# Selection columns inside another constant, and a 32-byte gap behind each page of on-chip memory

## The chip, the cores and the metric

The kernel runs on one core of a Trainium2 chip. It is one program for the core's five engines: TensorE (PE for its matmuls, PEld for its weight loads), VectorE (DVE), ScalarE (ACT), GpSimd (POOL) and SyncE (SP), which here only issues DMAs. The metric is device time in microseconds (us) of one execution, given as the median of several runs. A profile is one execution taken by the hardware profiler.

## The reference

A two-layer backbone over 1,024 latent tokens of width 1,024, with 256 context tokens ahead of them. All arrays are float32.

```python
for i in range(2):
    shift, scale, gate = split(silu(c) @ ada_w[i] + ada_b[i], 3)
    h = rmsnorm(x, norm_g[i]) * (1 + scale) + shift
    if i == 0:   # windowed grouped-query attention, 16 query heads, 4 key heads of 128
        q, k, v, z = split(h @ w_in)            # 1024 -> 2048 + 512 + 512 + 2048
        q, k = rope(q), rope(k)
        o = softmax([sink, q @ k_ctx, q @ k_window]) @ [v_ctx, v_window]   # |i - j| <= 128
        y = (o * silu(z)) @ w_out               # 2048 -> 1024
    else:        # convolution module
        a, gl, z = split(h @ w_in + b_in, 3)    # 1024 -> 3 * 2048
        u = depthwise_conv31(a * sigmoid(gl)) + dw_b
        y = (silu(layernorm(u) * g + b) * silu(z)) @ w_out
    x = x + gate * y
return rmsnorm(x) * final_g
```

## The kernel before, in words

Every large matrix product is done in the `float32r` type of TensorE with the operands split into a high and a low part: `hi = round(full)`, `lo = full - hi`. One product is then three matmuls into the same accumulator: high with high, high with low, low with high (`mm3`). In each of them one operand is stationary (128 by 128, loaded ahead of the matmul) and the other streams through (mostly 128 partitions by 512 columns, 2,048 bytes in each partition).

Nearly all of these operands live in 45 **pages**: buffers of 1,024 float32 values (4,096 bytes) in each of the 128 partitions, handed out by `pg = Pages(pgpool, 45, "page", 1024)`. Six smaller buffers of 528 values (2,112 bytes), `hp = Pages(pgpool, 6, "half", 528)`, hold intermediate rows. A freed page goes to the end of the line of free ones, so that the same page holds one after another a raw weight block (`wraw`), its high or low part (`whi`, `wlo`), a part of the normalised input (`hh`, `hl` in the first layer, `h2h`, `h2l` in the second), queries, keys, values, probabilities (`p`), or a part of the gated branch output (`ozh`, `ozl`, `gs`) or of an output weight block (`woh`, `wol`).

```python
def alloc(self, dt, shape=None, name="pg"):
    i = self.free_.popleft()
    t = self.pool.tile([P] + list(shape or [self.words]), dt, tag=f"{self.tag}{i}",
                       name=f"{name}_{self.tag}_{self.count}", bufs=1)
```

A page gets its place in a partition when its tag is used for the first time, behind what was placed before it; each buffer takes a multiple of 32 bytes. Constants come first (`ctile`): the identity `ident`, `vt` (128 by 128, a table of per-channel vectors, of which columns 0 to 111 are used), `sel` (128 by 2: two columns of zeros and ones), `sink`, `nsink`, `ones`, `dww`, then `pthi` and `ptlo` (the transposed probabilities), small vectors, and then halves and pages.

`sel` is read by TensorE alone. In `ada_cols(pr)`, which runs four times within the first 60 us, four small matmuls add the four rows of a modulation product and turn them into columns: `PE.matmul(cps[:, 2 * i:2 * i + 2], rw[0:5, i * P:(i + 1) * P], sel[0:5], ...)`.

The stages in order: modulation products (`ada_mm`, with weights `araw`) and the first projections, bound by loads; the attention heads, each with its projections in the gaps (`gemm_half`: stationary `whi` or `wlo`, streaming `hh` or `hl`); the output projection of the first layer (`proj_attn`: stationary `ozh` or `ozl`, streaming `woh` or `wol`); the second layer's input projection (`b_mm`: stationary `whi` or `wlo`, streaming `h2h` or `h2l`) with the convolution on VectorE, GpSimd and ScalarE beside it; its output projection (`proj_out`: stationary `gs`, streaming `woh` or `wol`). The order of instructions on each engine comes from the tile framework's scheduler; TensorE's is the program's own.

Of the kernel before, what the change touches and what calls it, by code (L numbers as in the profile page):

```python
# [9 lines left out]
F32 = mybir.dt.float32  # L10
# [4 lines left out]
P = 128  # L15
# [38 lines left out]
class Pages:  # L54


    def __init__(self, pool, n, tag, words):
        self.pool, self.tag, self.words = pool, tag, words
        self.free_ = deque(range(n))
        self.at = {}  # L60
        self.count = 0

    def alloc(self, dt, shape=None, name="pg"):
        if not self.free_:
            raise RuntimeError(str([t[1].name for t in self.at.values()]))
        i = self.free_.popleft()
        self.count += 1
        t = self.pool.tile([P] + list(shape or [self.words]), dt, tag=f"{self.tag}{i}",
                           name=f"{name}_{self.tag}_{self.count}", bufs=1)
        self.at[id(t)] = (i, t)  # L70
        return t

# [22 lines left out]
def backbone_kernel(  # L95
# [23 lines left out]
    def nm(s):  # L119
        uid[0] += 1  # L120
        return f"{s}_{uid[0]}"
# [21 lines left out]
    def ctile(shape, dt, name):  # L143
        return cpool.tile(shape, dt, tag=name, name=name, bufs=1)
# [15 lines left out]

    ident = ctile([P, P], F32, "ident")
    vt = ctile([P, P], F32, "vt")
    sel = ctile([P, 2], F32, "sel")
    sink = ctile([P, NH], F32, "sink")
    nsink = ctile([P, NH], F32, "nsink")
    ones = ctile([P, P], F32, "ones")
# [1038 lines left out]
    for t in ("pthi", "ptlo"):  # L1205
        f = cpool.tile([P, 5, 528], F32, tag=t, name=nm("ubuf"), bufs=1)
# [520 lines left out]
```

## Time and profile before

| | us |
|---|---|
| median of 3 runs | 1757.55 |
| lowest and highest of them | 1756.67, 1760.27 |
| span of the profiled execution, first to last instruction | 1752.9 |
| PE busy in that span (8,420 matmul records) | 1720.7 |
| PEld, DVE, ACT, POOL busy | 1424.8, 1148.3, 889.4, 895.4 |

The page of the profile gives no time for the profiled execution but its span; the median lies 4.65 us above it, and that is taken as what lies around a span. "Idle before" in a row is idle time of the engine just before the instructions of that row, with what ended it. A matmul's record lasts longer than the time from its start to the next one's, since matmuls follow each other in a pipeline; so rates are read from the starts. In the chain of work that ended last, a row gives the start, the length and after "x" the number of instructions, so that length over number is the time for one.

### The profile page before, as it was taken

Reading aid. Unit: us, or ns where it says so; the run is one execution under the profiler, and the core shown is the slowest. Engines: PE = TensorE matmul, PEld = TensorE weight load, DVE = VectorE, ACT = ScalarE, POOL = GpSimd, SP = SyncE. Lnnn points to the kernel's source line nnn. Section 1 sums busy time; section 2 is a strip of 40 time slices with the busy share of each in tenths; the row PEclk is TensorE's granted clock in tenths of the full one; section 3 lists DMA queues with packets and bytes.
Section 4 is the critical chain, followed back from the end, with each engine's and each line's share of the span. In section 5 each row is a group of like instructions: output and inputs, shape, how many; then the busy total and the mean of one; then the engine's idle time right before and its main releaser. Section 6 shows DMA issues by size and latency. Waiting matters only on the chain.

```text
span 1752.9 us, 23877 instructions
## 1 busy us (share of the span) xinstructions
PE 1720.7 (98%) x8420; PEld 1424.8 (81%) x8420; DVE 1148.3 (66%) x2079; ACT 889.4 (51%) x1548; POOL 895.4 (51%) x705
## 2 busy tenths in 40 slices
PE   7999999999999999999999999999999999999997
PEld 4788888888888888888888888888888888788886
DVE  6755564556546563656315189999999999867823
ACT  7555553445345444545334355554665564466731
POOL 0245654566636565653101267998898888130300
PEclk9999999999999999999999999999999999999999
DMA  9334443444334542436777733011121202377971
GB/s 313 107 82 139 136 133 85 145 147 145 100 105 143 152 142 87 136 119 203 279 250 239 241 90 105 13 54 31 43 79 36 91 30 79 120 254 243 325 264 48
DMA packets 195324, 242.45 MB, mean 138 GB/s; under 512 B 11798, under 2 KB 126790, under 8 KB 195204
## 3 DMA queue, kind: packets, MB, share of 16 engines
q1 hardware_dynamic: 188516, 230.10, 40.3%
q10 hardware_dynamic: 6688, 10.83, 2.6%
q8 instruction: 66, 1.08, 0.3%
q14 instruction: 54, 0.44, 0.1%
HBM read 188.70 MB, written 41.69 MB: 131 GB/s over the span
## 4 chain that ended last, share of the span: by engine, by line
PE 86%; DMA 5%; DVE 3%; POOL 2%; ACT 2%; issue 2%; SPq 1%; ACTq 0%; POOLq 0%; DVEq 0%
PE psg L89 44%; PE pss L89 22%; PE pso L89 19%; DMA araw_page<-in_ada_w_dram 1%; POOL rope_half L89 1%; DMA low_page<-in_conv_w_out_dram 1%; DMA rope_half<-rope_half 1%; SPq L89 1%; DMA low_page<-in_attn_w_out_dram 1%; DMA wolC<-low_page 1%; DVE mask_page L89 1%; ACT p_page L89 0%; POOL wlo_page L89 0%; POOL low_page L89 0%; DMA wraw_page<-in_attn_w_in_dram 0%
## 5 line engine op out<-in xcount | busy, mean ns | idle before, releaser
L89 POOL TENSOR_TENSOR odd_half<-odd_half,prod_half 128x513 f32<-128x513 f32 (+2 forms) x252 | 312.8, 1250 | 24.2 <-ACT prod_half L89 11.0
L89 PE MATMUL psg<-hh_page,whi_page 128*128 128x512 f32 x600 | 237.6, 396 | 0.0
L89 PE MATMUL psg<-hh_page,wlo_page 128*128 128x512 f32 x600 | 236.9, 395 | 0.0
L89 PE MATMUL psg<-hl_page,whi_page 128*128 128x512 f32 x600 | 236.8, 395 | 0.0
L89 POOL TENSOR_TENSOR wlo_page<-wraw_page,whi_page 128x1024 fp32r<-128x1024 f32 x70 | 173.1, 2475 | 104.1 <-ACT whi_page L89 83.2
L89 ACT ACTIVATE prod_half<-ubuf,dww 128x513 f32<-128x513 f32 (+2 forms) x252 | 165.1, 674 | 107.3 <-POOL odd_half L89 105.1
L89 POOL TENSOR_SCALAR p_page<-p_page,sc 128x640 f32<-128x640 f32 (+1 forms) x128 | 100.8, 787 | 224.4 <-DVE sc L89 208.7
L89 PE MATMUL psg<-h2h_page,whi_page 128*128 128x512 f32 x464 | 183.9, 396 | 0.0
L89 PE MATMUL psg<-h2h_page,wlo_page 128*128 128x512 f32 x464 | 183.0, 394 | 0.0
L89 PE MATMUL psg<-h2l_page,whi_page 128*128 128x512 f32 x464 | 182.4, 393 | 0.0
L89 DVE SCALAR_TENSOR_TENSOR pss<-ubuf,dww,pss 128x512 f32<-128x512 f32 (+3 forms) x270 | 172.3, 670 | 0.1
L89 DVE SCALAR_TENSOR_TENSOR pss<-ubuf,wsum,pss 128x512 f32<-128x512 f32 (+3 forms) x270 | 171.7, 670 | 0.2
L89 DVE TENSOR_TENSOR ptlo<-pss,pthi 128x640 fp32r<-128x640 f32 (+1 forms) x144 | 103.3, 717 | 64.0 <-ACT pthi L89 62.8
L89 ACT ACTIVATE p_page<-p_page,sc 128x641 f32<-128x641 f32 (+1 forms) x128 | 102.7, 802 | 74.1 <-DVE sc L89 69.7
L89 ACT ACTIVATE pthi<-pss 128x640 fp32r<-128x640 f32 (+1 forms) x144 | 88.6, 615 | 91.7 <-PE pss L89 86.3
L89 PEld LDWEIGHTS psg<-hh_page,wlo_page 128*128 128x128 f32 x600 | 112.9, 188 | 26.3
L89 PEld LDWEIGHTS psg<-hh_page,whi_page 128*128 128x128 f32 x600 | 113.0, 188 | 20.8 <-DVE kvc_page L89 0.2
L89 PEld LDWEIGHTS psg<-hl_page,whi_page 128*128 128x128 f32 x600 | 112.9, 188 | 20.7
L89 ACT ACTIVATE whi_page<-wraw_page 128x1024 fp32r<-128x1024 f32 x88 | 92.6, 1053 | 69.0 <-PE psg L89 25.5
L89 PE MATMUL pso<-h2l_page,whi_page 128*128 128x512 f32 x304 | 119.9, 394 | 0.0
L89 PE MATMUL pso<-h2h_page,whi_page 128*128 128x512 f32 x304 | 119.8, 394 | 0.0
L89 PE MATMUL pso<-h2h_page,wlo_page 128*128 128x512 f32 x304 | 119.6, 394 | 0.0
(244 smaller groups left out, 4105.2 us busy)
## 6 DMA issues: line engine op xcount, KB each, us to landing
wraw_page<-in_conv_w_in_dram SPq DMA_DIRECT2D x48, 512.0 KB
wraw_page<-in_attn_w_in_dram SPq DMA_DIRECT2D x40, 512.0 KB
wol_page<-wolA SPq DMA_DIRECT2D x32, 512.0 KB
wo_page<-in_attn_w_out_dram SPq DMA_DIRECT2D x32, 512.0 KB
wo_page<-in_conv_w_out_dram SPq DMA_DIRECT2D x32, 512.0 KB
wol_page<-wolC SPq DMA_DIRECT2D x32, 512.0 KB
rope_half<-rope_half ACTq DMA_DIRECT2D x80, 128.0 KB
araw_page<-in_ada_w_dram SPq DMA_DIRECT2D x32, 256.0 KB
```

What stands on the lines that cost most here:

```text
L89: r = f(*a, **k)
```

## The change

The two columns of `sel` become columns 112 and 113 of the constant `vt`, which were unused. The DMA that fills them and the sixteen small matmuls that read them name `vt` instead of `sel`. And when a page's tag is used for the first time, a buffer of 8 float32 values (32 bytes), which nothing reads or writes, is placed behind the page.

```diff
@@ class Pages, __init__
         self.count = 0
+        self.shifted = set()
@@ class Pages, alloc
                            name=f"{name}_{self.tag}_{self.count}", bufs=1)
+        if self.tag == "page" and i not in self.shifted:
+            self.shifted.add(i)
+            self.pool.tile([P, 8], F32, tag=f"gap{i}", name=f"gap_{i}", bufs=1)
         self.at[id(t)] = (i, t)
@@ backbone_kernel
-    sel = ctile([P, 2], F32, "sel")
+    sel = vt[:, 112:114]
```

No instruction is added, removed or moved on any engine, and each waits for the same semaphores as before. What differs in the instructions is the one name. On SyncE's queue, at the program's start, before (`sel` is the selection constant, `crow` the condition vectors, `araw` the modulation weights):

```order
3 L89 DMA ident<-in_k_ident_dram 128x128
4 L89 DMA crow_half_75<-in_norm_g_dram 16x128
5 L89 DMA sel<-in_k_sel_dram 128x2
6 L89 DMA araw_page_92<-in_ada_w_dram 128x2x256 x2
7 L89 DMA araw_page_93<-in_ada_w_dram 128x2x256 x2
```

and now (the line number of the recording helper is 93 instead of 89, and buffer numbers are shifted by the gap buffers):

```order
3 L93 DMA ident<-in_k_ident_dram 128x128
4 L93 DMA crow_half_74<-in_norm_g_dram 16x128
5 L93 DMA vt<-in_k_sel_dram 128x2
6 L93 DMA araw_page_92<-in_ada_w_dram 128x2x256 x2
7 L93 DMA araw_page_94<-in_ada_w_dram 128x2x256 x2
```

The DMA stands in the same place with another destination. What the change does move is addresses. The built programs place the buffers so (bytes within a partition):

| | before | after |
|---|---|---|
| `pthi`, `ptlo` | 4832, 16096 | 4800, 16064 |
| first page, second, third, fourth | 34848, 41056, 45152, 49248 | 34816, 41056, 45184, 49312 |
| pages at a multiple of 64 | 0 of 45 | 23 of 45 |
| pages 32 behind a multiple of 64 | 45 of 45 | 22 of 45 |
| halves at a multiple of 64 | 0 of 6 | 5 of 6 |
| pages by address modulo 256, with 0, 32, 64, 96, 128, 160, 192, 224 | 0, 26, 0, 9, 0, 6, 0, 4 | 7, 6, 5, 6, 5, 4, 6, 6 |
| end of the last page | 227616 | 228992 |

Of the program's 8,362 matmuls 6,055 stream 512 columns. Over these, the addresses of the streaming operand and of its own stationary operand compare as follows:

| of 6,055 matmuls with 512 columns | before | after |
|---|---|---|
| streaming operand starts at a multiple of 64 | 0% | 50.5% |
| the two operands' addresses are equal modulo 256 | 30.6% | 11.2% |
| the two operands' addresses differ modulo 64 | 0.8% | 51.0% |

## The prediction, made before the changed kernel was run

> **What bounds the kernel now.** The head of the profile's page and its line of shares in the chain of work that ended last come first.
>
> ```profile
> span 1752.9 us, 23877 instructions
> PE 1720.7 (98%) x8420; PEld 1424.8 (81%) x8420; DVE 1148.3 (66%) x2079; ACT 889.4 (51%) x1548; POOL 895.4 (51%) x705
> PE   7999999999999999999999999999999999999997
> PEclk9999999999999999999999999999999999999999
> PE 86%; DMA 5%; DVE 3%; POOL 2%; ACT 2%; issue 2%; SPq 1%; ACTq 0%; POOLq 0%; DVEq 0%
> ```
>
> TensorE's matmuls are busy for 1720.7 of 1752.9 us, at the full clock, in every slice but the first and the last, and 86% of the chain is theirs. No other engine is above 66%, and the weight loads fill 81%. So the time is set by how soon one matmul can follow another. That is read next from the chain, whose long pieces are unbroken runs of matmuls with 512 columns: start, length, engine, output, line and count.
>
> ```profile
> 977.41 44.47 PE pss L89 x192
> 1047.61 33.33 PE psg L89 x144
> 1500.09 27.78 PE psg L89 x120
> ```
>
> Length over count is 231.6, 231.5 and 231.5 ns. The clock cannot explain any difference from run to run here, since it is granted in full throughout. But single stretches differ. The timeline of TensorE around 984 us (part of the first piece above) and around 831 us gives starts and lengths:
>
> ```profile
> 984.00 0.39 PE L89 MATMUL pss<-woh_page,ozl_page 128*128 128x512 f32 x1
> ...
> 986.94 0.39 PE L89 MATMUL pss<-woh_page,ozh_page 128*128 128x512 f32 x1
> 831.02 0.40 PE L89 MATMUL psg<-wol_page,ozh_page 128*128 128x512 f32 x1
> ...
> 833.35 0.40 PE L89 MATMUL psg<-woh_page,ozl_page 128*128 128x512 f32 x1
> ```
>
> In the first stretch 13 starts take 2.94 us, 226.2 ns each; in the second 10 take 2.33 us, 233.0 ns each. The operation is the same, and so are shape, operand kinds and neighbours. What differs is where the operands lie. In the first stretch all four pages (two of streaming weights, two stationary) start 32 bytes behind a multiple of 256. In the second the streaming pages do so too, but both stationary ones start 96 behind one. So 6.8 ns, 3%, hangs on the lowest bits of addresses when they stay the same for several matmuls. That is the only thing this change touches.
>
> The slowest regular spacing is in the input projection of the second layer:
>
> ```profile
> 1379.49 0.40 PE L89 MATMUL psg<-h2l_page,whi_page 128*128 128x512 f32 x1
> 1379.72 0.40 PE L89 MATMUL psg<-h2h_page,wlo_page 128*128 128x512 f32 x1
> 1379.96 0.39 PE L89 MATMUL psg<-h2h_page,whi_page 128*128 128x512 f32 x1
> ```
>
> The second start to the third is 0.24 us, against 0.23 from the first to the second.
>
> **The change part by part.** No instruction is added, removed or moved, so every term is a change in duration.
>
> *VectorE, ScalarE, GpSimd.* The convolution reads one buffer at many offsets, tap by tap, and the tile view shows what an offset does to a duration (minimum, median, maximum in ns):
>
> ```profile
> L89 ACT ACTIVATE prod_half<-ubuf,dww x49: 707/727/732, 1170.0 to 1259.7; 128x513 f32<-128x513 f32 x49
> L89 DVE SCALAR_TENSOR_TENSOR pss<-ubuf,dww,pss x27: 734/740/750, 1169.5 to 1218.1; 128x512 f32<-128x512 f32 x27
> L89 PE MATMUL pso<-sel,arow_half x32: 245/247/268, 16.4 to 59.6; 5*128 5x2 f32 x32
> ```
>
> The taps start at offsets that differ by 4 or 8 bytes, so that starts on, 32 behind and anywhere between multiples of 64 are among them; the medians lie within 2% of both ends on VectorE and 3% on ScalarE. GpSimd has no such row; it takes the same 0. What hides an error of 2% is that these engines are not the bound. In the convolution's stages it can be seen by the windows view (length, then busy time and count of PE, PEld, DVE, ACT and POOL, clock, DMA share, GB/s):
>
> ```profile
> 0.00:40.00 40.00, 31.85 (x126) 18.31 (x127) 23.91 (x42) 28.83 (x35) 0.92 (x7) 0.96 0.98 308
> 990.00:1480.00 490.00, 490.00 (x2136) 398.47 (x2135) 447.33 (x722) 278.21 (x401) 407.11 (x299) 1.00 0.20 61
> ```
>
> TensorE is busy for all of 490.00 us; VectorE has 42.67 us to spare, 9.5% of its work. Term: 0. Without this cover 2% of 447.33 would be 8.9 us.
>
> *The selection columns.* Thirty-two of the recorded small matmuls, at 245 to 268 ns in the row above, all within the first 60 us. If the operand's new place changed each by as much as they differ among themselves (23 ns), it would be 0.7 us either way; taken 0.
>
> *Loads.* In the second window above the transfer engines are busy for 0.20, and a load there has slack. In the first 40 us they are busy for 0.98 and the loads lead. The chain's share for the window from 0 to 45 us, and the pieces of three such loads:
>
> ```profile
> by line: DMA araw_page<-in_ada_w_dram 53.9%; SPq L89 27.8%; issue 5.9%; PE pso L89 4.8%; DVE alo_page L89 2.7%; DVE hf_page L89 1.8%; ACT hh_page L89 1.7%; ACTq L89 0.1%; ACT ahi_page L89 0.1%; DVE hl_page L89 0.1%; DVEq L89 0.0%
> 15.91 7.07 DMA araw_page<-in_ada_w_dram
> 27.19 6.19 DMA araw_page<-in_ada_w_dram
> 33.40 5.10 DMA araw_page<-in_ada_w_dram
> ```
>
> 53.9% of 45 us is 24.3 us of transfers into pages. Their pieces spread by 7.07 − 5.10 = 2 us though every destination is 32 behind a multiple of 64. I take 0 for the new destinations and ±2 us as bounds.
>
> *TensorE, the one term with a size.* Of the 6,055 matmuls with 512 columns, the streaming and the stationary operand now start equal modulo 256 in 30.6%, and afterwards in 11.2%: 19.4 points, 1,176 matmuls. If each of them loses what the steady stretches show, 1,176 × 6.8 ns = 8.0 us are added. That is the upper bound. The lower one comes from the chain's own pieces: by the addresses, the piece at 977.41 has 42% of its matmuls with equal operands and the piece at 1047.61 has 18%, and they run at 231.6 and 231.5 ns. Where the classes alternate from matmul to matmul, as they mostly do, the share does nothing. So 0 to 8 us; I take 2, because the long mixed pieces are the nearer rows, and the changed kernel's sequences are mixed still more. Only a steady run, like the one at 984 us, can lose the full 6.8 ns.
>
> The bounds do not cover what is new: half of the streams (50.5%) start at a multiple of 64, and half of the pairs (51.0%) differ by an odd multiple of 32. In the trace of before nearly all 512-column streams start 32 behind one, and only 0.8% of the pairs differ modulo 64. Those are the modulation products, whose stationary condition columns lie 0, 16 or 48 behind a multiple of 64:
>
> ```profile
> 30.27 0.40 PE L89 MATMUL pso<-alo_page,c 128*4 128x512 f32 x1
> ...
> 33.05 0.40 PE L89 MATMUL pso<-alo_page,c 128*4 128x512 f32 x1
> ```
>
> Twelve starts in 2.78 us are 231.7 ns each, just the common rate. That speaks for no new price, though with a stationary operand of only 4 columns. The weight loads, mean 188 ns in the row below (instructions, busy us, mean ns), fit under 231 with 43 ns to spare, so a load that is slower by a fifth still stays hidden.
>
> ```profile
> L89 PEld LDWEIGHTS psg<-hh_page,whi_page 128*128 128x128 f32 x600 | 113.0, 188 | 20.8 <-DVE kvc_page L89 0.2
> ```
>
> The Trainium skill, in "SBUF — State Buffer", section "Specifications (TRN2)", gives 16-byte lines in that memory, with a penalty for crossing into a new one; both the old and the new starts lie on such a line, so by it alone nothing would change. The two rates at 984 and 831 us, whose starts are all on such lines, show that this is not the whole of it.
>
> Sum: 0 + 0 + 0 + 2 us on a span of 1752.9 us. The median of the runs lies 4.65 us above that span, at 1757.55, and I carry these over unchanged: 1757.55 + 2 = 1759.6 us.
>
> **The rivals.** A difference of 0.2%, 3.5 us, is about what a measurement of this kernel can tell from none; the three runs of before span 3.6 us.
>
> *Half of the streams run at the better rate (faster).* If the common loss comes from starting 32 behind a multiple of 64 (nearly every 512-column stream did), those that now start at one run at 226.2 instead of 231.5 ns: 5.3 ns × 3,058 = 16 us, 1741.5. If the alternation frees both halves, it is twice that, 32 us, 1725.5. For it: 226.2 occurs, so the engine can do it, and no other work stands in the way. Against it: in the stretch at 984 us the streams start 32 behind and yet run at the best rate.
>
> The Trainium skill, in "TensorE: Matmul & The Clock Gate", section "Back-to-back issue gap", gives N/2.4 + 2.5 ns for isolated warm matmuls, which is 215.8 ns for 512 columns; no stretch here reaches it. Half of the streams at that rate would make this rival's gain an estimated 48 us.
>
> *Pairs that differ by 32 collide (slower).* Two operands that lie 64 apart modulo 256 cost 6.8 ns more than equal ones; a half step could cost more again. Priced at the slowest regular spacing, 0.24 us to the two digits shown and 241 by the trace's nanoseconds, 9.5 ns × 3,088 (51.0% of 6,055) is 29 us: 1786.9. It decides from 1.1 ns for each such pair, where it passes 3.5 us. For it: closeness in the low bits is what helps, and the change takes it away. Against it: the modulation products, at 231.7 ns.
>
> *The addresses even out (no change).* Successive matmuls already mix four classes modulo 256, and mixing eight gives the same mean: 1757.6 us.
>
> **How the numbers follow.** The forecast, with its own range from 1757.5 to 1765.6, has 0.40: between a loss of 0 and of 8 us, about half of it on each side of 3.5 us (0.22 slower, 0.18 same). The even mixture has 0.05, all same. The better rate has 0.33, since a new class of streams is half of the work and nothing but its untested rate speaks on it. The collision has 0.22, less because one row of pairs that differ shows no price. Faster 0.33; same 0.18 + 0.05 = 0.23; slower 0.22 + 0.22 = 0.44. The likeliest single figure is 1759.6. The range must take in most of both outer cases: down to 1728, just short of both halves gaining, and up to 1786, just short of the full collision. What lies outside is the last of either, about 0.1 at each end.
>
> **What would show it.** Right: the same counts of instructions, VectorE, ScalarE and GpSimd busy within 1% of before, PE at full clock, and long pieces of the chain between 231.5 and 233 ns per matmul, with steady stretches of 226 become rare. The better rate would show in those pieces as 226 to 229 ns, above all where streams start at multiples of 64; the collision as 234 ns and more where the operands differ by an odd multiple of 32. Idle time on TensorE of more than now, or a first 45 us that ends over 2 us earlier or later, would say that the loads or the other engines do feel the addresses, and my zeros were wrong.

## The result, and the profile after

The changed kernel takes 1756.3 us (median of 12 runs, 1753.8 to 1759.96), the kernel before 1757.31 us beside it (12 runs, 1754.05 to 1760.51). The ratio is 1.0001, with a 95% interval from 0.9994 to 1.0009; it is not simply the quotient of these two medians, which is 0.9994, the lower end of that interval. Either way no change can be told. The forecast was 1759.6 us, 2 us more than before. "Same", the outcome that came, had the smallest of its three chances, 0.23.

The head of the page of the changed kernel, to be held against the lines of before:

```profile
span 1753.1 us, 23877 instructions
PE 1722.7 (98%) x8420; PEld 1423.6 (81%) x8420; DVE 1144.2 (65%) x2079; ACT 889.6 (51%) x1548; POOL 895.1 (51%) x705
PEclk9999999999999999999999999999999999999999
```

The counts are the same. VectorE, ScalarE and GpSimd are busy for the same time within 0.4%, as the zeros for them had it. TensorE has 2 us more. The long pieces of its chain (start, length, engine, output, line, count), in the changed kernel:

```profile
975.77 44.42 PE pss L93 x192
1045.92 33.35 PE psg L93 x144
1499.17 27.83 PE psg L93 x120
1579.81 27.88 PE pss L93 x120
```

Before they were 44.47, 33.33, 27.78 and, below, 27.78 us. So the first is 0.1% shorter, the others are 0.1 to 0.4% longer; for one matmul that is 231.4, 231.6, 231.9 and 232.3 ns. Two more pieces of before say where it stood in time:

```profile
457.02 14.00 PE psg L89 x72
...
1580.50 27.78 PE pss L89 x120
```

and the piece in the changed kernel that answers to the first of them:

```profile
455.48 14.00 PE psg L93 x72
```

The changed kernel is 1.54 us ahead at 457 us, 0.69 us ahead at 1580, and 0.2 us behind at the end. From 457 us to the end it lost 1.7 us, and a quicker start covered it. Whether that start belongs to the change is asked below.

In each profile some 5,950 matmuls with 512 columns have a start that follows at once on another's. Their mean spacing, worked out from all these starts, is 231.73 ns before and 231.98 ns after. 0.25 ns × 5,950 is 1.5 us, where the prediction put 2.

### The profile page after: what moved, and what is told of

Read it like the earlier page. It is cut to its first block, busy times and chain, and to the rows that moved or that the text cites. A ratio compares the mean times of both kernels' runs of the same rounds, so it can differ in the third digit from the quotient of the medians.

```text
span 1753.1 us, 23877 instructions
## 1 busy us (share of the span) xinstructions
PE 1722.7 (98%) x8420; PEld 1423.6 (81%) x8420; DVE 1144.2 (65%) x2079; ACT 889.6 (51%) x1548; POOL 895.1 (51%) x705
## 4 chain that ended last, share of the span: by engine, by line
PE 86%; DMA 6%; DVE 2%; POOL 2%; ACT 2%; issue 1%; SPq 1%; ACTq 0%; POOLq 0%; DVEq 0%
PE psg L93 45%; PE pss L93 22%; PE pso L93 19%; DMA araw_page<-in_ada_w_dram 1%; POOL rope_half L93 1%; DMA low_page<-in_conv_w_out_dram 1%; DMA wraw_page<-in_attn_w_in_dram 1%; DMA rope_half<-rope_half 1%; SPq L93 1%; DMA low_page<-in_attn_w_out_dram 1%; DMA x_page<-in_x_dram 0%; ACT p_page L93 0%; POOL wlo_page L93 0%; DMA wo_page<-in_conv_w_out_dram 0%; DMA wolC<-low_page 0%
## 5 line engine op out<-in xcount | busy, mean ns | idle before, releaser
L93 PE MATMUL psg<-hh_page,wlo_page 128*128 128x512 f32 x600 | 236.4, 394 | 0.0
L93 PE MATMUL psg<-hl_page,whi_page 128*128 128x512 f32 x600 | 236.4, 394 | 0.0
```

Of the source, the lines that this page charges most:

```text
L93: r = f(*a, **k)
```

## The experiments

The theory: the spacing of the matmuls is set by where the streaming and the stationary operand lie to each other in the low bits of their addresses, but the good case pays only when it lasts for several matmuls. Rivals: each pair counts by itself; a place at a multiple of 64 has its own price; or addresses are not the cause at all.

**Spacing measured by itself.** A kernel of matmuls alone, each from two buffers at chosen offsets:

```python
PE.matmul(acc[t], stat[:, 8 * w:8 * w + P], stream[:, 8 * s:8 * s + N], start=True, stop=True)
```

> Leaves out the whole backbone: 4,250 matmuls with 512 streamed columns alone, in blocks of 24 with fixed addresses, the streaming and the stationary operand each at 0, 32, ..., 224 bytes from a common place (64 combinations, run twice in different orders), then 96 each with one place throughout, with places that step by 64, and with places that step by 32, then a dozen blocks beside VectorE copies and two dozen beside loads. Theory of the prediction (the low bits of the two addresses set the spacing, and mixtures average): blocks with equal places near 226 ns, others near 233, the same in both orders; the two mixed stretches within 1 ns of each other. Rival A (a difference of an odd multiple of 32 collides): such blocks at 234 to 241 ns, the stretch stepping by 32 slower by over 2 ns. Rival B (addresses are not the cause; the spacing depends on what else goes on or on how a stretch begins): with TensorE alone no order by place, the same block differs between the two orders by as much as blocks with different places do, and the blocks beside copies or loads are slower.

The windows view, one window for each block of 24 (from the first start to the start of the next block; then busy time and count of PE, PEld, DVE, ACT, POOL, clock, DMA share, GB/s; PE's count includes the neighbours at the edges). First the differences streaming minus stationary of 0, 32, 64, 96, 128 and 160 bytes:

```profile
12.85:18.29 5.44, 5.44 (x26) 4.50 (x24) 0.00 (x0) 0.00 (x0) 0.00 (x0) 1.00 0.00 0
18.29:23.89 5.60, 5.60 (x25) 4.50 (x24) 0.00 (x0) 0.00 (x0) 0.00 (x0) 1.00 0.00 0
23.89:29.39 5.50, 5.50 (x25) 4.51 (x24) 0.00 (x0) 0.00 (x0) 0.00 (x0) 1.00 0.01 3
29.39:35.01 5.62, 5.62 (x26) 4.51 (x25) 0.00 (x0) 0.00 (x0) 0.00 (x0) 1.00 0.00 0
35.01:40.60 5.59, 5.59 (x25) 4.50 (x24) 0.00 (x0) 0.00 (x0) 0.00 (x0) 1.00 0.00 0
40.60:46.22 5.62, 5.62 (x25) 4.51 (x24) 0.00 (x0) 0.00 (x0) 0.00 (x0) 1.00 0.00 0
```

Divided by 24: 226.7, 233.3, 229.2, 234.2, 232.9 and 234.2 ns; since the windows are given to 0.01 us, these are good to about 0.5 ns, and the figures that follow are worked out from the trace's nanoseconds. Without the first four of each block, over all 64 combinations in the first order, equal places have 226.6 to 226.9 ns at every one of the eight places, and a difference of 32 has 233.3 at every one. So the difference counts, not the place. Of the odd multiples of 32, 32 and 224 have 233 ns, as 128 and 192 mostly do; 96 and 160 are the slowest, but only by up to 1 ns (233.6 and 234.3). In the second order equal places have 227.2 to 228.0 ns, since most of these blocks follow one at another place and begin with up to nine uneven starts before they are at 226 to 227; "the same in both orders" held for the ranking and not to the nanosecond. A difference of 64 is the unsteady one: 228.9 in the first order, and either 228.7 to 228.9 or 233.3 in the second: 233.3 through the whole block where the block before was 96 apart, 229 where it was 64 apart. Next a difference of 32 beside VectorE copies, equal places beside loads, and a difference of 32 beside loads:

```profile
809.17:814.77 5.60, 5.60 (x26) 4.50 (x24) 5.36 (x8) 0.00 (x0) 0.00 (x0) 1.00 0.00 0
859.32:864.79 5.47, 5.47 (x26) 4.51 (x24) 0.00 (x0) 0.60 (x1) 0.00 (x0) 1.00 0.61 228
875.75:881.35 5.60, 5.60 (x26) 4.50 (x24) 0.00 (x0) 0.00 (x0) 0.00 (x0) 1.00 1.03 410
```

The difference of 32 has the same 5.60 us as with TensorE alone, beside copies and beside loads at 410 GB/s, and equal places 5.47: VectorE's copies and the loads don't enter. The rival that addresses are not the cause falls. So does the collision as it was priced: of the odd multiples of 32 only 160 reaches the 234 ns that it asked for, and none comes near 241. Of the two mixed stretches, 95 starts took 21.90 us stepping by 64 and 22.08 us stepping by 32, 230.5 and 232.4 ns: not within the 1 ns that the theory expected and just short of the rival's 2 ns, so a mixture's mean does depend a little on its classes.

**All pages at one place.** From the kernel before:

```diff
-    hp = Pages(pgpool, 6, "half", 528)
+    hp = Pages(pgpool, 6, "half", 576)
```

> The kernel before with halves of 2,304 bytes, so that all 45 pages lie at the same place modulo 256 (160, that is 32 behind a multiple of 64): 95.9% of the 512-column matmuls have equal operands modulo 256, against 30.6%. If equal operands are worth 6.8 ns each, 65.3% of 6,055 x 6.8 ns = 27 us less, ratio 0.985. If mixtures average and equal ones pay only in steady runs, all runs are steady here, and the same 27 us go. If addresses are not the cause: within 0.2% of the kernel before, long pieces of the chain at 231.5 ns.

It takes 1733.41 us against 1756.52; ratio 0.9872 (0.9858 to 0.9885), by which it is 22.5 us less. The chain's long pieces in it:

```profile
969.78 43.52 PE pss L89 x192
1038.79 32.68 PE psg L89 x144
1482.18 27.25 PE psg L89 x120
```

226.7, 226.9 and 227.1 ns for one matmul. The expected 27 us came out at 22.5: the base was 231.7 and not 233, so the step was 4.1 ns in the mean (231.73 to 227.60) over 5,950 matmuls, 24.6 us, of which the time shows 22.5. Addresses are the cause, then; but "each pair by itself" and "only steady runs pay" both had 27 us here, so this run doesn't tell them apart.

**The same at a multiple of 64.** The run above with `sel = vt[:, 112:114]`.

> As the run with all pages at one place modulo 256, and with the selection columns in the other constant, so that this place is 128 modulo 256, a multiple of 64. If a start at a multiple of 64 runs at the better rate: 16 us per half of the streams, 32 us less than with the pages 32 behind one. If only the difference of the two operands counts: the same time as that run, ratio 0.985. If addresses are not the cause: within 0.2% of the kernel before.

1733.9 us, ratio 0.9874 (0.9861 to 0.9888), mean spacing 227.51 ns: the same as 32 behind a multiple of 64. A start at a multiple of 64 has no rate of its own.

**The two parts of the change apart.** The gaps without the selection columns:

> The change without its first part: the selection columns keep their own constant, the gaps stay. 23 pages then lie 32 behind a multiple of 64 and 22 at one, the other way round than in the changed kernel; the shares of pairs that are equal modulo 256 or differ modulo 64 are the same as there. If the difference of the operands counts or nothing does: within 0.2% of the changed kernel and of the kernel before. If the absolute place counts, constants and halves included: up to 1% away from the changed kernel.

1756.99 us, ratio 1.0007 (0.9998 to 1.0016). And the selection columns without the gaps:

> The change without its second part: the selection columns go into the other constant, no gaps. All pages move by 32 bytes to multiples of 64, and the differences between operands stay as before (30.6% equal modulo 256). If only differences and their order count: within 0.2% of the kernel before, mean spacing of 512-column matmuls 231.7 ns. If a place at a multiple of 64 has a price or a gain of its own: 2 ns or more away from that, 12 us.

1754.82 us, ratio 0.9992 (0.9981 to 1.0002). Neither can be told from the kernel before. Their windows from 990 to 1480 us, with TensorE busy throughout, first of the gaps alone, then of the selection columns alone:

```profile
990.00:1480.00 490.00, 490.00 (x2132) 397.14 (x2131) 450.43 (x726) 278.52 (x401) 408.98 (x300) 1.00 0.20 60
```

```profile
990.00:1480.00 490.00, 490.00 (x2135) 397.89 (x2135) 446.43 (x722) 279.23 (x402) 406.59 (x298) 1.00 0.20 62
```

2,132 and 2,135 matmuls, where before had 2,136. The mean spacings are 231.95 and 231.71 ns, against 231.98 in the changed kernel and 231.73 before: the small rise of the spacing comes with the gaps, and moving every page by 32 bytes does nothing.

**Which sequences pay.** Matmuls alone again, in sequences.

> Leaves out the backbone again: matmuls with 512 streamed columns alone. First sequences of period two, each in two forms: own operands equal and the next one's stationary operand elsewhere, and own operands apart by 32, 64, 128, 96 or 160 bytes but the next one's stationary operand equal. Then random sequences of 192 in which a share of 0, 0.3, 0.6, 0.8, 0.9 and 1 of the matmuls has both operands at one place and the rest are anywhere in eight places; then fully random places that differ by multiples of 32, of 64 and of 128; then equal and unequal ones in runs of 24 and in turn; then differences of 4 to 28 and of 256 and 512 bytes. If a matmul's own pair sets its spacing: first form 226.7, second 233; random sequences on a straight line from 233 to 226.7 ns; runs of 24 and turn by turn both at 230. If it is the pair of the stream and the weights being loaded under it, for the next matmul: the second form is the fast one. If a steady state of several matmuls is needed, as the prediction has it: both forms near 231 to 233, the line bent, with 232 or more at 0.3 and at 0.6, 230 at 0.8, and runs of 24 at 230 against 232 or more turn by turn.

Windows of 192 matmuls each (start of the first to start of the next sequence). The first six have shares of equal pairs of 0.16, 0.36, 0.66, 0.79, 0.91 and 1 as drawn; the last two have one half equal, in runs of 24 and turn by turn:

```profile
123.28:167.87 44.59, 44.59 (x194) 36.08 (x193) 0.00 (x0) 0.00 (x0) 0.00 (x0) 1.00 0.00 0
167.87:212.43 44.56, 44.56 (x194) 36.05 (x193) 0.00 (x0) 0.00 (x0) 0.00 (x0) 1.00 0.00 1
212.43:256.82 44.39, 44.39 (x193) 36.05 (x192) 0.00 (x0) 0.00 (x0) 0.00 (x0) 1.00 0.00 0
256.82:301.20 44.38, 44.38 (x193) 36.05 (x192) 0.00 (x0) 0.00 (x0) 0.00 (x0) 1.00 0.00 1
301.20:345.24 44.04, 44.04 (x193) 36.04 (x192) 0.00 (x0) 0.00 (x0) 0.00 (x0) 1.00 0.00 0
345.24:388.79 43.55, 43.55 (x194) 36.04 (x193) 0.00 (x0) 0.00 (x0) 0.00 (x0) 1.00 0.00 1
...
522.15:566.51 44.36, 44.36 (x194) 36.07 (x193) 0.00 (x0) 0.00 (x0) 0.00 (x0) 1.00 0.00 1
566.51:610.67 44.16, 44.16 (x193) 35.97 (x192) 0.00 (x0) 0.00 (x0) 0.00 (x0) 1.00 0.00 0
```

232.2, 232.1, 231.2, 231.1, 229.4 and 226.8 ns. From 0.16 to 0.79 only 1.1 ns are gained, from 0.79 to 1 another 4.3: the line is bent as a steady state makes it, and not straight as pairs that count by themselves would have it. The trace shows it start by start. In the four sequences from 0.36 to 0.91, unequal pairs follow at 232.2 ns, the first equal pair of an unbroken run at 231.6, the second and third at 231.2, the fourth to tenth at 230.0, and from the eleventh on 227.8. The three sequences of random places that step by 32, 64 and 128 gave 231.9, 231.5 and 231.3 ns. Pairs in period two gave 228.4 to 234.0 ns in the form with equal own operands and 229.9 to 231.6 in the other, so neither pair rules alone: where both operands step together between two places 32 bytes apart, every pair is equal, and the spacing is still 232.1 ns.

The theory's own numbers were met at 0.3 alone. It had 232 at 0.6 and got 231.2, 230 at 0.8 and got 231.1, runs of 24 at 230 and got 231.0, and the period-two forms within 231 to 233, which they left on both sides. Turn by turn it had 232 or more and got 230.0, less than the runs of 24; that is what the rival of single pairs had. Why a regular alternation averages its two pairs where a random mixture does not is not shown.

**Two doses in the kernel.** Halves of 576 and one gap of 160 bytes behind the 23rd page (43% of the pairs equal):

> The kernel with halves of 2,304 bytes and one gap of 160 bytes behind the 23rd page, so that pages lie at two places modulo 256: 43% of the pairs are equal, 55% differ by an odd multiple of 32. If time falls in proportion to the share of equal pairs (1756.5 us at 31%, 1733.4 us at 96%, so 0.354 us a point): 1752.3 us, ratio 0.9976. If equal pairs pay only in unbroken runs (a third power of the share as a rough guide): 0.08 against 0.03 and 0.88, so 1755 us, ratio 0.9993.

1758.71 us, ratio 1.0014 (1.0006 to 1.0023). With the gap behind the fifth page instead (76%):

> The same with the gap of 160 bytes behind the fifth page: five pages at one place modulo 256, forty at another, 76% of the pairs equal. In proportion to the share: 1740.5 us, ratio 0.9909. If only unbroken runs pay (third power: 0.44 against 0.03 and 0.88): 1745 us, ratio 0.9936.

1744.24 us, ratio 0.9935 (0.9923 to 0.9948). Proportion to the share had 0.9976 and 0.9909, both outside the intervals; the third power had 0.9993 and 0.9936. The second is met. The first is missed: 0.9993 lies below the interval, and the run was slower than that by 0.0021, 3.7 us. 56% of its pairs differ by an odd multiple of 32, nearly all by 96 or 160, which the kernel of matmuls alone showed as the slowest differences (233.6 and 234.3 ns), and its mean spacing is 232.25 ns. In its trace the pairs 96 apart follow at 232.8 ns (2,420 of them) and those 160 apart at 232.2 (883), where the unequal pairs of the kernel before have 231.9; that makes an estimated 2.4 us of the 3.7. No run tested it, and the rest is open.

**The transposed probabilities too.** All pages at one place, with 64 bytes ahead of them:

```diff
+    ctile([P, 16], F32, "pad")
```

> All pages at one place modulo 256, and 64 bytes ahead of them, so that the transposed probabilities lie at that place too: 99.0% of the 512-column pairs are equal, against 95.9%. If the 195 pairs of probabilities, at 231.9 ns in the run without this, come to 227.4: 0.9 us less than there, ratio to the kernel before 0.9867. If their waits rather than their spacing set the time of the heads: the same as there, 0.9872.

1733.56 us, ratio 0.9868 (0.9853 to 0.9883): the two expectations differ by less than the interval, so the time is inconclusive. The spacing of those pairs did come down, to 226.9 ns by the trace. All three kernels of this kind beat the kernel before and the changed one by 1.3%.

**Whose is the quicker start?** Second profiles of both kernels.

> The changed kernel once more, for a second profile. If the 1.2 us by which the first profile is ahead of the one before at 71 us come from the new places of the loads: again about 70.4 us there. If they are chance of the start: anywhere from 69.5 to 71.7. The mean spacing at 232.0 ns either way.

> The kernel before once more, for a second profile. If its later arrival at that place, 71.6 us, is a property of the kernel, again 71.6; if it is chance, anywhere from 69.5 to 71.7. The mean spacing at 231.7 ns either way.

The spans are 1755.3 us for the changed kernel and 1753.0 for the one before. The 251st of the program's matmuls starts at 71.13 us in this changed profile and 70.50 in this one of before; in the first pair it was 70.42 and 71.64. Over the other kernels it lies between 69.69 and 71.43. So the start is chance, not the change. The spacing is not: 231.94 and 231.74 ns, as the first time (231.98 and 231.73).

Part of that chance is the clock. The window from 40 to 50 us of the first pair, before and then the changed kernel, has TensorE's granted clock as the third number from the end:

```profile
40.00:50.00 10.00, 7.79 (x33) 4.66 (x31) 7.44 (x8) 8.63 (x14) 1.28 (x1) 0.83 0.88 320
40.00:50.00 10.00, 9.00 (x45) 5.80 (x43) 7.74 (x11) 8.12 (x14) 1.30 (x1) 1.00 0.81 315
```

In the trace of before, starts of 512-column matmuls, elsewhere 0.23 us apart, are 0.42 us apart for some 3.4 us of that window: half the clock for a third of it, as the 0.83 says. In its first 70 us the kernel before has two such stretches in the first pair and the changed kernel one; in the second pair it is the other way round, and each time the kernel with two arrives later. It is not the only cause, since a kernel with one of them (all pages at a multiple of 64) arrives at 71.43 us.

## Why the prediction came out as it did

*The bound.* TensorE's spacing sets the time; everything else at zero. Right: with all pages at one place VectorE, ScalarE and GpSimd are busy for the same time within 0.8%, and the time moved by 22.5 us with the spacing.

*The clock.* "Granted in full throughout" was a misreading: the prediction's own window for the first 40 us has 0.96, and the trace of before has two stretches at half the clock in its first 50 us. The long stretches that it compared, at 1.00, are not touched by that, but differences of 1 or 2 us from run to run can be the clock's.

*The 4.65 us around a span.* They were taken as what every execution has beyond its span. But the time of each run lies only 1.74 to 1.86 us above that run's own span. So the profiled execution of before was a quick one, by nearly 3 us. The forecast starts from the median and is not changed by it.

*Equal operands are the good case.* Right, and by the size read from two short stretches of the profile: 6.8 ns there, 6.6 ns in the kernel of matmuls alone (226.7 against 233.3). It holds for places that stay the same from matmul to matmul, which is how the prediction put it.

*Equal pairs in a mixture pay nothing, so 0 to 8 us with 2 taken.* Right in kind. The step rested on two chain pieces with 42% and 18% of equal pairs and nearly the same 231.6 and 231.5 ns, and the random sequences show that flat part (0.1 ns from 0.16 to 0.36). The traces and addresses of the two kernels show where the loss lay. Before, equal pairs follow at 231.7 ns as the first to third of an unbroken run (1,578 of them), at 229.2 as the fourth to ninth (134), and at 226.8 from the tenth on (103); unequal pairs follow at 231.9. That is 1.2 us in all, most of it in those 237 matmuls. In the changed kernel 646 equal pairs have 231.8 ns, and only nine stand tenth or later. The term measured 0.25 ns × 5,950 = 1.5 us in the first pair of profiles and 0.20 × 5,950 = 1.2 in the second. The time did not show it: 1.5 us is under 0.1% of it, and the interval reaches from 1 us less to 1.6 us more. The 2 us were picked inside the bounds of 0 and 8 and not worked out, so that they came this near is in part luck; and the range, 1728 to 1786 us, was wide enough to hold most outcomes.

*Half of the streams at the better rate.* Wrong, and it had a chance of 0.33. Its own counter-argument, that the best stretch of before started 32 behind a multiple of 64, was decisive: both places give 227.5 to 227.6 ns when all pages share them. In the changed kernel half of the streams start at a multiple of 64, and the mean spacing rose.

The Trainium skill, in "TensorE: Matmul & The Clock Gate", section "Wait — 56ns, not 53.3ns?", has 215.7 ns for 512 columns as measured from start to start. No sequence here reached it, with TensorE alone included; the best was 226.6 ns, with two float32r operands.

*Odd multiples of 32 collide.* Wrong at that price: 233.3 ns at a difference of 32. The price of 241 ns was the slowest moment of a mixture, not a state. A small part of it is there: in the changed kernel's trace the pairs that differ by an odd multiple of 32 follow at 232.2 ns and the other unequal ones at 231.6, which is 0.7 ns and under the 1.1 ns at which the prediction had it decide. "Closeness in the low bits is what helps" was wrong as well: a difference of 4 bytes has 236.4 ns.

The Trainium skill, in "SBUF — State Buffer", section "Specifications (TRN2)", has lines of 16 bytes. All page starts lie on such lines, and the pairs still differ by 6.6 ns, so lines alone do not give the spacing.

*The loads and the selection columns.* Zero, with ±2 and ±0.7 us. Up to the 251st matmul the profiles differ by 2 us (69.69 to 71.64) whatever the kernel, and that covers whatever these are; so these zeros are not refuted, and no run shows them by themselves.

What stays open is why equal low bits help. The runs give the rates for each difference, not the part of the memory or of the engine in which the time is lost.

## What to carry to other kernels

When one engine's back-to-back rate sets the time, read that rate over short stretches and ask what differs between the fast and the slow ones; here 3% lay in addresses, which no line of the profile's page names. A benefit that needs a steady state does not scale with the share of good cases: going from 31% to 11% of equal pairs cost 1.2 to 1.5 us of spacing, which the time did not show, and going to 96% gave 22.5 us. So where operands stream past each other like this, try the version in which every buffer has the same low address bits before shuffling buffers; here it was one constant.

## What had not been expected of the hardware

With fixed operands the spacing of 512-column float32r matmuls changes when one start address moves by a single word. In the kernel of sequences the stationary operand stayed in place, and streams that start 4, 8, 12, 16, 20, 24 and 28 bytes behind it gave 236.4, 233.2, 228.8, 231.7, 240.0, 233.4 and 226.6 ns (24 matmuls each, the first four left out), and 256 and 512 bytes 227.2 and 226.7. So equality is not the only good case: 28 bytes have the best rate too. Whether it is the difference or the stream's own start that counts below 32 bytes was not tested. After a switch of places an equal pair takes several matmuls to settle: the 256-byte block begins with 224, 231, 236, 228, 233 and 231 ns, and stays at 226 to 227 from there on, and blocks of the first kernel that came from another place needed up to nine. That fits with scattered equal pairs paying so little.
